# Sliding-window attention inside a weight-streaming trunk: one transposed tile for two triangles of probabilities, three banks for the queries, and sums, scaling and masks on GpSimd

## The chip, the cores and the metric

One Trainium2 chip, one of its cores. The kernel is launched once. The metric is the device time in microseconds of one execution; what stands as "time" is the median over several runs, and one further execution was taken by the profiler. The engines are named as the profile names them: PE is TensorE's matrix products and PEld its weight loads, DVE is VectorE, ACT is ScalarE, POOL is GpSimd, SP issues the DMAs.

## What is computed

Two layers over 256 tokens of width 2048: a recurrent layer with its feed-forward part, then one projection to shared keys and values, then an attention layer with its feed-forward part. The change lies in the attention. Cut to that:

```python
SEQ, D_MODEL, HEAD_DIM, N_HEADS, N_KV_HEADS, WINDOW, BLOCK = 256, 2048, 64, 32, 4, 128, 128

def attn_block(x, g, w_q, q_g, sinks, w_o, k_band, v_band):
    h = rms_norm(x, g)
    q = rms_norm((h @ w_q).reshape(bsz, s, N_KV_HEADS, GROUP, HEAD_DIM), q_g)
    scores = einsum("bnqhgd,bnkhd->bnhgqk", q, k_band) / sqrt(HEAD_DIM)
    scores = where(mask, scores, NEG_INF)      # 0 <= q_pos - k_pos < 128, k_pos exists
    probs = softmax(concatenate([scores, sink], -1), -1)[..., :-1]
    out = einsum("bnhgqk,bnkhd->bnqhgd", probs, v_band)
    return x + out.reshape(bsz, s, N_HEADS * HEAD_DIM) @ w_o
```

With 256 tokens there are two blocks of 128 queries. Queries of block 0 see their own block's keys up to themselves: a lower triangle. Queries of block 1 see their own block's lower triangle and, of block 0's keys, those fewer than 128 back: the strictly upper triangle. The two triangles of block 1 fill a 128x128 square between them without overlap.

## The kernel before

**The products.** All weights stream from HBM in jobs of 128x1024 float32 (two k-tiles of 128 by four feature tiles of 128). ACT rounds a job to `hi` (L259), DVE forms the remainder `lo` (L260), and PE adds `hi`·x_hi, `hi`·x_lo and `lo`·x_hi into PSUM (`products`, L289 to 325). A product of 128 columns of weights with 256 tokens is called narrow here; a job is 24 narrow products. Where a feature tile owns a whole PSUM bank of 512 columns ("wide"), one 512-column product can do `hi`·x_hi and `hi`·x_lo at once; `products` places runs of three of those at chosen points (after other work on PE, and in jobs named by `SYNC`). There are 704 jobs. Buffers are four deep, and the split of a job is emitted three jobs ahead (`stream`, L271).

**Groups and banks.** PSUM has eight banks. `group` (L340) runs the jobs of four feature tiles and then hands the banks to `done`, which empties them. For the queries (`w_q`, four groups of eight jobs) a group holds four banks, three of them wide (`wide=3`). For the first two groups of `w_o` four feature tiles share two banks (`paired`) and the jobs of both groups are interleaved: six jobs of the first, six of the second, then two and two (`late=2`, L492 to 505).

**The attention visits.** Everything beside the job stream is generators that `run_bg` steps between half jobs (a tick is half a job). `pairs` (L926 to 977) makes *visits*: 16 pairs of heads pass through a pipeline, each pair being two heads of 64 rows in one 128-partition tile. In a visit PE does up to three things for three different pairs, in this order: V, the product of values with transposed probabilities (`values`, L861); T, the transposes of probabilities (`transposes`, L873, six of 128x128); S, the scores (`scores`, L881). A pair has its scores in visit i, its transposes in visit i+2 and its values in visit i+3. All these go through `pe_other` (L327). Between them, `softmax` (L892) runs on DVE and ACT: masked maximum (L900), exponentials with their sums, the reciprocal of the sum, and four scalings on DVE (`ts`, L131), two per head. After T, ACT copies the transposes from PSUM into two tiles (a 128x512 and a 128x256 copy). A visit takes up to four banks from the eight, at most `MISC` = 4 may be out, and none starts while `hold` is set, which is in a group's last two jobs (L360). When the job stream needs a result that is not there (`need`, L213), it steps the generators until it is, with no job between.

**The queries' finish.** The task in `attn` (L987 to 1031) squares the queries, sums them per head on PE, transposes, computes the scales, and queues four pairs per group.

## Time and profile before

| | |
|---|---|
| median of 3 runs | 1990.1 us (1989.94 to 1990.55) |
| profiled execution: span | 1988.6 us |
| PE busy / PEld busy | 1982.0 us (100%) / 1935.5 us (97%) |
| DVE busy | 1271.2 us (64%) |
| ACT busy | 1067.9 us (54%) |
| POOL busy | 0.2 us, 4 instructions |
| HBM read | 371.88 MB, 188 GB/s over the span |

The execution's own device time beside its span is not listed; the median stands 1.5 us above the span, which is the part of an execution that lies outside the first and the last instruction. In the span's 40 slices PE shows nine tenths or more in each and the granted PE clock is full in each. The attention stage, from the first scores to the last values, lies at about 1072 to 1210 us. Matmul rows overlap in the trace, so what a product costs is read from the distance between the starts of two rows and not from the length of one.

### The profile page before, as it was taken

The numbers are of one execution on the slowest core, as the hardware profiler recorded it, in microseconds if no ns is written. First come the engines' busy times: TensorE is split into PE (matmuls) and PEld (weight loads), VectorE is DVE, ScalarE is ACT, GpSimd is POOL, SyncE is SP. The second block draws the span as 40 slices with busy tenths as digits, with TensorE's granted clock in tenths as the row PEclk, the third lists the DMA queues.
The fourth block names the chain that finished last, engine by engine and source line by source line (L and its number), as shares of the span: only waits on it lengthen the run. The fifth ranks groups of instructions, "written<-read, shape, count | busy, mean of one in ns | idle before, by whom it ended". The sixth has DMA issues, their size and how long they took to land.

```text
span 1988.6 us, 40066 instructions
## 1 busy us (share of the span) xinstructions
PE 1982.0 (100%) x16684; PEld 1935.5 (97%) x16684; DVE 1271.2 (64%) x2049; ACT 1067.9 (54%) x1624; POOL 0.2 (0%) x4
## 2 busy tenths in 40 slices
PE   9999999999999999999999999999999999999999
PEld 9999999999999999999999889999999999999999
DVE  8988876556556655545668786755565565554453
ACT  7798655444444444444556775544454454444442
POOL 0000000000000000000000000000000000000000
PEclk9999999999999999999999999999999999999999
DMA  8555655565556555556555435565566656656663
GB/s 279 185 187 182 211 191 192 196 196 191 192 195 196 191 192 196 195 191 194 197 186 167 134 101 163 188 197 195 191 193 196 195 191 194 197 193 203 204 208 128
DMA packets 105302, 376.58 MB, mean 189 GB/s; under 512 B 11808, under 2 KB 14240, under 8 KB 105120
## 3 DMA queue, kind: packets, MB, share of 16 engines
q1 hardware_dynamic: 104832, 373.88, 57.8%
q8 instruction: 130, 2.13, 0.4%
q14 instruction: 52, 0.43, 0.1%
q10 hardware_dynamic: 288, 0.14, 0.0%
HBM read 371.88 MB, written 2.10 MB: 188 GB/s over the span
## 4 chain that ended last, share of the span: by engine, by line
PE 99%; ACT 0%; DVE 0%; DMA 0%; issue 0%; ACTq 0%
PE b L323 94%; PE b L334 2%; PE b L641 1%; PE b L331 1%; PE b L832 1%; ACT s L113 0%; PE b L321 0%; PE b L841 0%; PE b L842 0%; PE b L843 0%; DMA x<-in_x 0%; DVE s L131 0%; DVE lo L260 0%; ACT L113 0%; DVE s L122 0%
## 5 line engine op out<-in xcount | busy, mean ns | idle before, releaser
L323 PE MATMUL b<-s,hi 128*128 128x256 f32 (+1 forms) x10276 | 1431.9, 285 | 0.4 <-ACT s L113 0.4
L323 PEld LDWEIGHTS b<-s,hi 128*128 128x128 f32 x10276 | 1313.4, 188 | 30.4 <-ACT s L113 0.7
L260 DVE TENSOR_TENSOR lo<-raw,hi 128x1024 fp32r<-128x1024 f32 (+1 forms) x705 | 861.4, 1223 | 651.2 <-ACT hi L259 648.1
L259 ACT ACTIVATE hi<-raw 128x1024 fp32r<-128x1024 f32 (+1 forms) x705 | 745.7, 1059 | 817.7 <-PE b L323 756.7
L323 PE MATMUL b<-s,lo 128*128 128x256 f32 x5504 | 831.8, 277 | 0.0
L323 PEld LDWEIGHTS b<-s,lo 128*128 128x128 f32 x5504 | 720.4, 188 | 2.4 <-issue 0.8
L113 ACT ACTIVATE s<-h 128x256 fp32r<-128x256 f32 (+1 forms) x106 | 40.8, 411 | 23.8 <-DVE h L122 23.8
L113 ACT ACTIVATE t<-b 128x256 f32<-128x256 f32 x136 | 49.8, 374 | 2.5 <-PE b L323 0.3
L113 ACT ACTIVATE s<-x,par 128x256 fp32r<-128x256 f32 x80 | 38.6, 499 | 19.3 <-DVE x L122 13.6
L113 ACT ACTIVATE s<-s 128x256 f32<-128x256 f32 (+1 forms) x112 | 39.6, 409 | 5.7 <-DVE s L126 5.5
L113 ACT ACTIVATE h<-h 128x256 f32<-128x256 f32 (+1 forms) x104 | 38.8, 375 | 2.1
L113 ACT ACT_TABLE_LOAD x30 | 38.5, 1283 | 0.5
L126 DVE SCALAR_TENSOR_TENSOR s<-x,par,s 128x256 fp32r<-128x256 f32 x80 | 37.5, 482 | 1.4 <-ACT s L113 0.8
L122 DVE TENSOR_TENSOR h<-b,rstd 128x256 f32<-128x256 f32 x100 | 37.6, 417 | 0.0
L122 DVE TENSOR_TENSOR x<-x,b 128x256 f32<-128x256 f32 x64 | 24.1, 418 | 21.0 <-PE b L323 21.0
L113 ACT ACTIVATE s<-s,h 128x128 f32<-128x128 f32 x64 | 28.3, 443 | 13.3 <-DVE h L131 13.2
L122 DVE TENSOR_TENSOR h<-h,rstd 128x256 f32<-128x256 f32 x94 | 35.4, 419 | 0.0
L122 DVE TENSOR_TENSOR h<-h,h 128x256 f32<-128x256 f32 x88 | 35.0, 420 | 0.4 <-ACT h L113 0.4
L122 DVE TENSOR_TENSOR s<-h,s 128x256 fp32r<-128x256 f32 x88 | 35.2, 420 | 0.1
L122 DVE TENSOR_TENSOR h<-b,t 128x256 f32<-128x256 f32 x92 | 34.6, 417 | 0.0
L122 DVE TENSOR_TENSOR s<-s,s 128x256 fp32r<-128x256 f32 (+1 forms) x80 | 30.9, 422 | 3.5 <-ACT s L113 3.5
L334 PE MATMUL b<-s,s 64*128 64x256 f32 (+3 forms) x292 | 29.0, 302 | 0.1
(99 smaller groups left out, 566.4 us busy)
## 6 DMA issues: line engine op xcount, KB each, us to landing
raw<-in_ffn_in SPq DMA_DIRECT2D x352, 512.0 KB, 3.5
raw<-in_ffn_out SPq DMA_DIRECT2D x176, 512.0 KB, 4.3
raw<-in_lru_in SPq DMA_DIRECT2D x63, 512.0 KB, 3.6
raw<-in_lru_out SPq DMA_DIRECT2D x32, 512.0 KB, 3.7
raw<-in_w_q SPq DMA_DIRECT2D x32, 512.0 KB, 3.3
raw<-in_w_o SPq DMA_DIRECT2D x32, 512.0 KB, 3.3
raw<-in_gate SPq DMA_DIRECT2D x8, 512.0 KB, 3.9
raw<-in_kv SPq DMA_DIRECT2D x8, 512.0 KB, 4.3
```

Source lines behind the costliest of these rows:

```text
L113: self.nc.scalar.activation(out, in_, func, **kw)
L122: self.nc.vector.tensor_tensor(out, a, b, op)
L126: self.nc.vector.scalar_tensor_tensor(out, a, s, b, op0, op1)
L259: self.nc.scalar.activation(hi[:, q], raw[:, q], AF.Copy)
L260: self.nc.vector.tensor_tensor(lo[:, q], raw[:, q], hi[:, q].bitcast(F32), ALU.subtract)
L323: self.nc.tensor.matmul(*args, **kw)
L331: self.other = self.ins(f(*args, **kw))
L334: self.other = self.ins(f(*args, **kw))
L641: nc.tensor.matmul(out[j], (hi if high else lo)[:, c:c + P], x2[kt][:, q:q + T], start=kt == 0 and high > q, stop=kt == 1 and not high)
L832: nc.tensor.matmul(ps[f][:, 0:T], w0, x2[kt][:, q:q + T], start=k0 + kt == 0 and high > q, stop=k0 + kt == ND - 1 and not high)
```

## The change

It has seven parts, all in the attention stage.

1. **One tile for two triangles.** After the exponentials, POOL adds the two halves of block 1 (columns 128 to 255 and 256 to 383) into the first of them, for each head (L925 of the changed kernel). The four scalings move from DVE to POOL, each now 128x128 (L929). `transposes` makes four transposes rather than six.
2. **Masks after the transposes.** ACT copies one 128x512 tile from PSUM rather than that and a 128x256 one. POOL multiplies its block-1 half by two 0/1 masks from the constants (L971): once into a second tile (own block), once in place (previous block). Both are products of 128x256 elements. V reads both tiles.
3. **Order in a visit.** V, S, T where it was V, T, S. The pacing credits to `run_bg` go from 900/700/900 to 800/900/450 ns.
4. **Even visits.** While pairs are still to come, a visit waits for a new pair rather than running with the old ones alone.
5. **Three banks.** `w_q` groups use two wide banks and one bank shared by the other two feature tiles (`packed`); `MISC` goes to 5, and `hold` is set for one job before the end of a packed group and not at all in a paired one.
6. **`w_o` interleaved.** The jobs of its first two groups alternate one by one.
7. **Constants.** 256 more columns (the two masks).

```diff
-K_HS, K_MASK = 640, 672
-NCON = 672 + 384
+K_HS, K_MASK = 640, 672
+K_PREV, K_OWN = 672 + 384, 672 + 512
+NCON = 672 + 640
...
-    MISC = 4
+    MISC = 5
...
+                    elif packed:
+                        ps = [self.bank() for _ in range(3)]
+                        st["ps"] = [(ps[0], True, 0, 1), (ps[1], True, 1, 1)]
+                        st["ps"] += [(ps[2][:, f * T:f * T + T], False, 2, f) for f in range(2)]
+                        st["bank"] = ps
...
-                elif c >= nk // 2 - 2:
+                elif c >= nk // 2 - (1 if packed else 2) and not paired:
                     self.hold = True
...
-                    n = nk // 2 - late
-                    self.jobs += first[0][:n] + first[1][:n] + first[0][n:] + first[1][n:]
+                    self.jobs += [j for both in zip(*first) for j in both]
...
             for hh in (1, 0):
-                for j in (2, 1, 0):
-                    o = ps[0][:, hh * T + j * P:hh * T + j * P + P] if j < 2 else ps[1][:, hh * P:hh * P + P]
+                for j in (1, 0):
+                    o = ps[0][:, hh * T + j * P:hh * T + j * P + P]
                     self.pe_other(o, sc[hh][:, j * P:(j + 1) * P], one, f=nc.tensor.transpose)
...
             for hh in range(2):
-                for b, c0, c1 in blocks:
+                o = sc[hh][:, P:2 * P]
+                nc.gpsimd.tensor_tensor(o, o, sc[hh][:, 2 * P:3 * P], ALU.add)
+                for b in range(2):
                     i = b * 2 + hh
-                    o = sc[hh][:, c0:c1]
-                    self.ts(o, o, den[:, i:i + 1], None, ALU.mult)
+                    o = sc[hh][:, b * P:b * P + P]
+                    nc.gpsimd.tensor_scalar(o, o, den[:, i:i + 1], None, ALU.mult)
...
-                elif not (A or B or C):
+                elif n < ND or not (A or B or C):
                     yield 1
                     continue
...
                     values(A[0], A[1], pt[1])
-                    self.pe(900)
+                    self.pe(800)
+                if new:
+                    scores(new[0], new[1], ps)
+                    self.pe(900)
                 if B:
                     transposes(B[1], pt)
-                    self.pe(700)
-                if new:
-                    scores(new[0], new[1], ps)
-                    self.pe(900)
+                    self.pe(450)
...
                     self.a(s[0], pt[0])
-                    self.a(s[1][:, 0:T], pt[1][:, 0:T])
+                    for o, c in ((last, K_OWN), (dst, K_PREV)):
+                        m = con[:, c:c + P].unsqueeze(1).broadcast_to([P, 2, P])
+                        nc.gpsimd.tensor_tensor(o, dst, m, ALU.mult)
```

In the programs' instruction order, a full visit on PE before, in the third group of `w_q`. Rows whose product reads two `s` tiles and writes 64 rows are V, those that read `con` are T, those with 128 rows from `s_11041` are S; those with `hi` or `lo` are the job stream.

```order
L323 MATMUL b_90<-s_11180,lo_82 128x256
L331 MATMUL b_86<-s_11935,s_11045 64x256
L334 MATMUL b_86<-s_11935,s_11045 64x256
L334 MATMUL b_86<-s_11936,s_11045 64x128 x2
L334 MATMUL b_86<-con,s_11792 128x128
L334 MATMUL b_85<-con,s_11792 128x128 x2
L334 MATMUL b_86<-con,s_11791 128x128
L334 MATMUL b_85<-con,s_11791 128x128 x2
L334 MATMUL b_87<-s_11041,s_11628 128x128
L334 MATMUL b_84<-s_11041,s_11628 128x128
```

The same place on the same engine in the changed program: V, then the last of the twelve score products, then T, then the job stream.

```order
L335 MATMUL b_89<-s_12217,s_11045 64x128 x2
L335 MATMUL b_90<-s_11042,s_11977 128x128
L335 MATMUL b_83<-s_11042,s_11977 128x128
...
L335 MATMUL b_90<-s_11042,s_11977 128x256
L335 MATMUL b_83<-s_11042,s_11977 128x256
L335 MATMUL b_84<-con,s_12140 128x128 x2
L335 MATMUL b_84<-con,s_12139 128x128 x2
L324 MATMUL b_86<-s_11240,hi_77 128x256 x2
```

Six transposes into two banks have become four into one, and they stand between the scores and the job stream rather than between values and scores.

On POOL, which before had no instruction of the attention, each visit now gives it eight. The rows of one period: two masks for the pair that was just transposed (L971), then for the pair whose exponentials are running two sums (L925) and four scalings (L929), then the next visit's masks.

```order
L971 TENSOR_TENSOR s_12217<-s_12216,con 128x256
L971 TENSOR_TENSOR s_12216<-s_12216,con 128x2x128
L925 TENSOR_TENSOR s_12224<-s_12224 128x128
L925 TENSOR_TENSOR s_12225<-s_12225 128x128
L929 TENSOR_SCALAR s_12224<-s_12224,h_96 128x128 x2
L929 TENSOR_SCALAR s_12225<-s_12225,h_96 128x128 x2
L971 TENSOR_TENSOR s_12302<-s_12301,con 128x256
L971 TENSOR_TENSOR s_12301<-s_12301,con 128x2x128
```

On DVE these four rows are gone from each softmax.

```order
L131 TENSOR_SCALAR s_12149<-s_12149,h_95 128x128
L131 TENSOR_SCALAR s_12149<-s_12149,h_95 128x256
L131 TENSOR_SCALAR s_12150<-s_12150,h_95 128x128
L131 TENSOR_SCALAR s_12150<-s_12150,h_95 128x256
```

In the first jobs of `w_o`, PE before: the last products of one visit's scores are followed at once by the values of the next visit, without a job between. There are three such doubled visits, with 24 narrow products between one double and the next.

```order
L334 MATMUL b_83<-s_11043,s_12243 128x256
L334 MATMUL b_85<-s_11043,s_12243 128x256
L334 MATMUL b_87<-s_12790,s_11045 64x256 x2
L334 MATMUL b_87<-s_12791,s_11045 64x128 x2
L334 MATMUL b_87<-con,s_12676 128x128
```

In the changed program 36 narrow products stand between the transposes of one visit and the values of the next in this stage:

```order
L335 MATMUL b_90<-con,s_12740 128x128 x2
L324 MATMUL b_89<-s_12306,hi_78 128x256 x4
L324 MATMUL b_84<-s_12221,lo_82 128x256 x2
...
L324 MATMUL b_85<-s_12567,lo_79 128x256 x2
L332 MATMUL b_83<-s_13005,s_11045 64x256
```

Over the whole stage there are as many visits as before, 19. In the changed program no two touch: between one visit's last product and the next one's first lie 36 narrow products (twelve times), 48 (three times, across a group's end) or 72 (three times, with the next queries' sums between). In `w_q`, where 9 visits fell before, 11 now fall. The runs of three wide products from the first queries' sums to the end of `w_q` are 19 where they were 32.

More of the change, by code (lines that the diff above doesn't have):

```diff
@@ L338, in ins, with group @@
         return getattr(i, "ins", i)
-    def group(self, src, nk, xs, done, last=False, sync=(), paired=False, jobs=None, wide=2):
+    def group(self, src, nk, xs, done, last=False, sync=(), paired=False, jobs=None, packed=False):
         st = {}
@@ L353, in mm @@
                         st["bank"] = ps
+                    elif packed:
[3 more added lines that the diff above has]
+                        st["bank"] = ps
                     else:
                         ps = [self.bank() for _ in range(4)]
-                        st["ps"] = [(p, bool(sync) and f < wide, f, 1) for f, p in enumerate(ps)]
+                        st["ps"] = [(p, bool(sync) and f < 2, f, 1) for f, p in enumerate(ps)]
                         st["bank"] = ps
@@ L378, in mm @@
                     todo = [(k, f, p) for g, q in order for k in range(2) for f in g for p in q]
-                self.products(todo, st, hi, lo, x2, c == nk // 2 - 1, keep, paired)
+                self.products(todo, st, hi, lo, x2, c == nk // 2 - 1, keep, paired or packed)
                 if last:
@@ L490, in residual, with project @@
         self.spawn(task())
-    def project(self, w, nk, xs, gains, r, out=None, late=0):
+    def project(self, w, nk, xs, gains, r, out=None, late=False):
         first = [[], []]
@@ L1032, in done @@
                 self.spawn(task())
-            self.group(lambda c, g=g: w[g, c], ND, xs, done, g == 3, self.SYNC, wide=3)
-        self.project(self.d["w_o"], ND, at, gains, rn, late=2)
+            self.group(lambda c, g=g: w[g, c], ND, xs, done, g == 3, self.SYNC, packed=True)
+        self.project(self.d["w_o"], ND, at, gains, rn, late=True)
     def run(self):
@@ L1092, in constants @@
     con[:, K_MASK:K_MASK + 384] = np.concatenate([own, prev, own], axis=1)
+    con[:, K_PREV:K_PREV + P] = prev.T == 0
+    con[:, K_OWN:K_OWN + P] = own.T == 0
     return con
```

3 lines of the change are left out of this document (added).

## The prediction

> **What bounds the kernel now.** I read the page first, then the chain that ended last, then windows of the attention stage, then PE's timeline of single visits, and last the costs by form.
>
> ```profile
> span 1988.6 us, 40066 instructions
> PE 1982.0 (100%) x16684; PEld 1935.5 (97%) x16684; DVE 1271.2 (64%) x2049; ACT 1067.9 (54%) x1624; POOL 0.2 (0%) x4
> PE 99%; ACT 0%; DVE 0%; DMA 0%; issue 0%; ACTq 0%
> ```
>
> PE carries 99% of the chain. What lies beside PE is hidden; a microsecond of PE saved or added anywhere is a microsecond of the result. So the question is how long PE spends on attention visits, and whether anything new makes it wait there.
>
> ```profile
> 76.91 21.76 PE b L323 x192
> 1198.31 4.24 PE b L323 x36
> ```
>
> Two pieces of the chain, with start, length and count. In the job stream a narrow product costs 21.76/192 = 0.1133 us; in the attention stage, after other work on PE, 4.24/36 = 0.1178 us. So there are two paces 4.5 ns apart. 704 jobs of 24 narrow products are 16896 x 0.1133 = 1914 us, which the change leaves alone; about 75 us are open to discussion.
>
> ```profile
> 1093.00:1124.00 31.00, 30.94 (x241) 26.06 (x241) 23.21 (x74) 23.67 (x60) 0.00 (x0) 1.00 0.42 137
> 1155.00:1189.00 34.00, 32.23 (x298) 27.08 (x297) 28.91 (x121) 26.84 (x85) 0.00 (x0) 1.00 0.25 79
> 1189.00:1210.00 21.00, 21.00 (x184) 18.89 (x183) 12.56 (x32) 12.05 (x31) 0.00 (x0) 1.00 0.42 132
> ```
>
> Windows: length, then busy time of PE, PEld, DVE, ACT, POOL. In the middle window, the doubled visits at the start of `w_o`, DVE is busy 28.91 of 34 us and PE misses 1.8 us: there PE waits for DVE. In `w_q` DVE has 23.21 of 31 us (75%).
>
> **What a visit costs.** PE's timeline: start, length, line, form.
>
> ```profile
> 1106.27 0.43 PE L331 MATMUL b<-s,s 128*64 128x256 f32 x1
> ...
> 1107.07 0.88 PE L334 MATMUL b<-con,s 128*128 128x128 f32 x6
> 1107.88 0.96 PE L334 MATMUL b<-s,s 64*128 64x128 f32 x12
> 1108.77 0.50 PE L321 MATMUL b<-s,hi 128*128 128x512 f32 x1
> 1109.11 0.40 PE L323 MATMUL b<-s,hi 128*128 128x512 f32 x1
> ...
> 1196.63 0.43 PE L331 MATMUL b<-s,s 128*64 128x256 f32 x1
> ...
> 1197.44 0.87 PE L334 MATMUL b<-con,s 128*128 128x128 f32 x6
> 1198.07 0.71 PE L323 MATMUL b<-s,hi 128*128 128x256 f32 x4
> ...
> 1208.33 0.43 PE L331 MATMUL b<-s,s 128*64 128x256 f32 x1
> ...
> 1209.13 0.74 PE L323 MATMUL b<-s,hi 128*128 128x256 f32 x4
> ...
> 1077.63 0.32 PE L331 MATMUL b<-s,s 64*128 64x128 f32 x1
> ...
> 1078.52 0.50 PE L321 MATMUL b<-s,hi 128*128 128x512 f32 x1
> ...
> 1088.23 0.27 PE L331 MATMUL b<-con,s 128*128 128x128 f32 x1
> ...
> 1088.97 0.96 PE L334 MATMUL b<-s,s 64*128 64x128 f32 x12
> 1089.86 0.50 PE L321 MATMUL b<-s,hi 128*128 128x512 f32 x1
> ```
>
> From start to start: a full visit takes 2.50 us, V 0.80, T 0.81, S 0.89. V alone takes 0.80 and S alone 0.89, so those two are the same by themselves. T is not: followed by S it takes 0.81 (0.74 without V), followed by the job stream 1198.07 - 1197.44 = 0.63, which is six times 0.105. So T into S costs 0.11 to 0.18 for the turn, T into the job stream nothing. S into the job stream costs a further 0.11: after 1108.77 the next 512-column product comes 0.34 later, where two narrow products' time is 0.23. An old full visit is thus 2.61 us.
>
> **The change, part by part.**
>
> *Two transposes fewer and the new order.* New visit: V 0.80, S 0.89, T 4 x 0.105 = 0.42, and a turn from S into T. No row shows V into S or S into T. S into T lies between 0, if the turn is already in S's 0.89, and the 0.18 seen between T and S; I take the 0.11 that S costs before the job stream, because T has the job stream's shape (128*128) and follows or precedes it free. V into S lies between 0 and another 0.2 beyond V's 0.80. I take 0, since V's 0.80 already holds a turn into a full-array product. New full visit 2.22 us, bounds 2.1 to 2.5; saved 0.39, bounds 0.1 to 0.5. Thirteen full visits: 13 x 0.39 = **5.1 us**. The one visit with T and S alone goes from 1.63 + 0.11 to 0.89 + 0.11 + 0.42: **0.3 us**. The two with V and T alone lose two transposes each: **0.4 us**.
>
> *Even visits.* The three doubles now:
>
> ```profile
> 1160.77 0.43 PE L331 MATMUL b<-s,s 128*64 128x256 f32 x1
> ...
> 1165.75 2.15 PE L323 MATMUL b<-s,hi 128*128 128x256 f32 x16
> ...
> 1168.77 0.43 PE L331 MATMUL b<-s,s 128*64 128x256 f32 x1
> ...
> 1170.68 0.87 PE L334 MATMUL b<-con,s 128*128 128x128 f32 x6 [1.04 <-DVE s L131]
> ...
> 1175.36 2.16 PE L323 MATMUL b<-s,hi 128*128 128x256 f32 x16
> ...
> 1178.39 0.43 PE L331 MATMUL b<-s,s 128*64 128x256 f32 x1
> ...
> 1183.85 2.15 PE L323 MATMUL b<-s,hi 128*128 128x256 f32 x16
> ```
>
> They take 4.98, 6.59 and 5.46 us, with 0.11 after each: 17.36. Six single old visits would be 15.66. The transposes there wait for DVE's scaling (the 1.04 us is one such wait). With at least 36 narrow products, 36 x 0.1133 = 4.1 us, between visits, the excess of **1.7 us** goes. Interleaving `w_o` moves no work: each pair's result is needed 36 products or more after its values are made.
>
> *Three banks, fewer wide ones.* The number of products is the same. The runs of three wide products, after which the quicker pace returns, fall from 32 to 19 in the `w_q` stage, and the visits there rise from 9 to 11. If all of the stage's 516 narrow products from the first queries' sums on ran at the slow pace, that would be 516 x 0.0045 = 2.3 us; some of this is paid already. I take **+0.6 us**, bounds 0 and 1.5.
>
> *Off PE.* DVE loses four scalings in each softmax, ACT one copy per visit. Both are hidden now and stay so; the cover is PE's 4.1 us between visits, and the `lo` splits run two jobs ahead of their use. The larger constants are 128 KB more in SP's one DMA of them at job 8, under PE's stream; SP's queue is otherwise as before.
>
> *POOL, the new link.* A pair goes: scores, DVE, ACT, reciprocal on DVE, two sums and four scalings on POOL, T two visits later, copy on ACT, two masks on POOL, then V of the next visit. PE is in order: V waiting for a mask holds S, T and the job stream. The times:
>
> ```profile
> 1130.76 0.43 PE L331 MATMUL b<-s,s 128*64 128x256 f32 x1
> ...
> 1138.89 0.18 DVE L137 RECIPROCAL h<-h 128x4 f32<-128x4 f32 x1
> ```
> ```profile
> L260 DVE TENSOR_TENSOR lo<-raw,hi 128x1024 fp32r<-128x1024 f32 x35 | 42.8, 1222 | 7.5 <-ACT hi L259 6.1 <-PE b L334 1.4
> L113 ACT ACTIVATE s<-b 128x512 f32<-128x512 f32 x16 | 9.4, 587 | 0.0
> L131 DVE TENSOR_SCALAR s<-s,h 128x128 f32<-128x128 f32 x32 | 9.1, 284 | 0.5
> L122 DVE TENSOR_TENSOR s<-s,s 128x256 fp32r<-128x256 f32 x12 | 4.6, 424 | 0.4 <-ACT s L113 0.4
> ```
>
> Now the reciprocal is done 8.3 us after its visit begins. S comes 0.8 us earlier in a new visit (1.69 rather than 2.50 us at its end): 7.5 us. The next visit begins at 2.22 + 4.1 = 6.3, its copy is done at about 6.3 + 2.22 + 0.3 + 0.59 = 9.4 (0.3 for the way from PE to ACT, an estimate), and its masks, which stand behind the scalings in POOL's queue, must be done by 12.6, when the visit after it begins. No row prices POOL. By DVE's rows, 0.284 for a scaling and 0.424 for a mask, the chain is 7.5 + 4 x 0.284 = 8.6, then from 9.4 two masks to 10.3: 2.3 us to spare. Let POOL be q times as slow as these rows: 7.5 + q x (1.14 + 0.85) reaches 12.6 at q = 2.6. All of a period's work on POOL, with two sums at 0.284, is q x 2.55 us and fills a period of 6.3 us at q = 2.5. So up to about q = 2.4 this costs nothing. As the far bound I take DVE's operation on 128x1024, four times a mask's size: 1.222/0.424 gives q = 2.9. Between q = 1 and 2.9 I take a value below 2, nearest to the rows of the same shape, and allow **0.5 us** in all for chance waits.
>
> The Trainium skill (GPSIMD Engine Reference, § 3.1 Elementwise) gives a 2048-element fp32 addition as 1.96 times as long on GpSimd as on VectorE; by that, as an estimate, q would be 2 and the chain would end 1.1 us before PE needs it, so the sum would stand. No run here shows it yet.
>
> **The sum.** 5.1 + 0.3 + 0.4 + 1.7 - 0.6 - 0.5 = 6.4 us off the profiled 1988.6: 1982.2. The median lies 1.5 us above that execution's span: **1983.5 us**, 0.33% less. Its own range is 1980 (turns free, pace unchanged) to 1986.
>
> **Rivals.**
>
> *POOL is late (slower).* Place: the first V product of each visit that follows 36 narrow products, ten of them. What speaks for it: DVE's `lo` has two operands in SBUF and runs 1.5 times per period for 1.222 us each; if POOL cannot read while DVE does that, one mask or scaling waits up to 1.2 us, and the room of 12.6 - 7.5 = 5.1 us for 1.99q shrinks to 3.9, so that q = 2 is already the limit. Against it: the `lo` splits fall mostly where POOL waits for the exponentials. Once POOL fills the period, the period is 2.55q: at q = 2.9 it is 7.4 us, 1.1 us of waiting at each of ten visits, 11 us in all, and 1983.5 - 0.5 + 11 = **1994 us**. It outweighs the whole gain from q = 2.75 on (7.0 us of stalls), the same as before; slower by 0.2% from 2.9.
> The Trainium skill (SBUF — State Buffer, § SBUF: two separate sides) states such a rule: GpSimd and a VectorE operation with two SBUF inputs take a shared port pair in turn, and the loser blocks for the whole instruction. By it the reduced room above applies. The trace of before, with POOL idle, can't show it.
>
> *The turns cost the same and the groups' ends wait.* If changing the array's use costs what it did, only the two transposes go: a full visit saves 0.21, thirteen 2.7 rather than 5.1. And the visit 12 products after a group's end (three times) puts its scores into banks that DVE has just emptied: two adds of 0.42, perhaps behind a `lo` of 1.22, against 12 x 0.1133 + 0.80 = 2.2 us; up to 0.6 us each. Together 2.4 + 1.8: **1987.7 us**. For it: DVE at 75% there. Against: it has four scalings less to do per visit.
>
> *The change doesn't even out what PE waits for.* The stalls of 1.7 us move to other visits, the rest holds: **1985.2 us**.
>
> **How the numbers follow.** Forecast 0.60, POOL late 0.20 (about 0.12 of it beyond +0.2%, the rest within), turns and groups' ends 0.12, stalls moved 0.08. A measurement of this kernel tells 0.2%, 4 us, from no change: faster means under 1986.1, slower over 1994.1. Faster: 0.60 + 0.08 + a quarter of the 0.12 = 0.71; slower 0.12; within 0.17. The range runs from 1980 to 1989.5: it holds the forecast, the moved stalls, the dear turns and the mild part of POOL's lateness.
>
> **What would show it.** Right: a full visit of 2.2 us from V to the job stream; no PE wait on DVE's scaling; 36 products between visits; POOL's masks ending before V's first product; 64 transposes of probabilities on PE where there were 96. Wrong: PE waiting at V with POOL as releaser, visits of 3 us and more, or DVE's `lo` lengthened where POOL works; then the first rival holds. If visits take 2.4 us, the turns were mis-sized.

## The result, and the profile after

| | before | after |
|---|---|---|
| time, median of 11 runs each | 1990.52 us (1989.93 to 1992.39) | 1986.19 us (1985.44 to 1987.02) |
| ratio of the times | | 0.9979, 95% interval 0.9971 to 0.9987 |
| span of the profiled execution | 1988.6 us | 1985.0 us |

The change saves 0.21%, where 0.33% was forecast; no execution of the one kernel reaches those of the other. Of the saving that the prediction worked out, the larger part arrived, and some 3.7 us of it were spent again on new waits. First the page of the changed kernel (span, busy times, chain of waits), which answers to the first fence of the prediction.

```profile
span 1985.0 us, 40177 instructions
PE 1976.7 (100%) x16691; PEld 1934.5 (97%) x16691; DVE 1259.8 (63%) x1981; ACT 1063.6 (54%) x1608; POOL 94.0 (5%) x132
PE 97%; ACT 1%; DVE 1%; POOL 1%; issue 0%; DMA 0%; ACTq 0%; POOLq 0%
```

PE still carries the chain, but 97% rather than 99% of it, and POOL has a share. POOL's 94.0 us all lie in the attention stage. The windows of that stage, with the columns as before (length, then busy PE, PEld, DVE, ACT, POOL, then the granted PE clock):

```profile
1093.00:1124.00 31.00, 30.39 (x256) 26.65 (x254) 22.12 (x73) 22.55 (x62) 21.95 (x30) 1.00 0.39 125
1155.00:1189.00 34.00, 32.90 (x302) 29.68 (x300) 24.68 (x76) 26.66 (x75) 24.67 (x34) 1.00 0.39 125
1189.00:1210.00 21.00, 20.31 (x178) 18.43 (x179) 10.68 (x23) 11.06 (x24) 13.34 (x18) 1.00 0.48 142
```

Before, PE was short of its window only in the middle one, by 1.8 us. Now it misses 0.6, 1.1 and 0.7 us. DVE is relieved (24.68 against 28.91 in the middle window), and POOL is busy for about 70% of the first two. What PE waits for, in the view of waits (us in total, times, longest):

```profile
PE b L332 <- POOL s L971: 2.9, 4, 1.0
```

These are the first products of V, waiting for POOL's masks. PE's timeline shows a visit without and one with such a wait:

```profile
1108.02 0.43 PE L332 MATMUL b<-s,s 128*64 128x256 f32 x1
...
1109.70 0.66 PE L335 MATMUL b<-con,s 128*128 128x128 f32 x4
1110.11 0.48 PE L322 MATMUL b<-s,hi 128*128 128x512 f32 x1
1110.43 1.57 PE L324 MATMUL b<-s,hi 128*128 128x512 f32 x10
...
1115.17 0.43 PE L332 MATMUL b<-s,s 128*64 128x256 f32 x1 [0.61 <-POOL s L971]
```

V and S take 1109.70 - 1108.02 = 1.68 us, T 0.41, and the first 512-column product 0.32, which is 0.09 more than two narrow ones. A new full visit is 2.18 us against 2.61. Over the 19 visits, those that took longer than an unhindered one of their kind lost about 3.7 us together (worked out visit by visit from PE's single rows; the largest are 1.1 us at 1189, 0.76 at 1202, 0.68 at 1115 and 0.67 at 1149, all of them ahead of V). Without these the span would be 1981.3 us. This 1981.3 is the base of the ledger below.

Why POOL is late shows in the timeline of all engines ahead of the longest of these waits:

```profile
1183.08 3.32 POOL L929 TENSOR_SCALAR s<-s,h 128x128 f32<-128x128 f32 x4
...
1183.54 1.23 DVE L261 TENSOR_TENSOR lo<-raw,hi 128x1024 fp32r<-128x1024 f32 x1 [0.57 <-ACT hi L260]
...
1186.37 2.55 POOL L971 TENSOR_TENSOR s<-s,con 128x256 f32<-128x256 f32 x2
...
1187.13 1.21 DVE L261 TENSOR_TENSOR lo<-raw,hi 128x1024 fp32r<-128x1024 f32 x1
...
1188.97 0.43 PE L332 MATMUL b<-s,s 128*64 128x256 f32 x1 [1.02 <-POOL s L971]
```

Four scalings take 3.32 us, two masks 2.55, and a `lo` split of DVE runs inside each stretch. The costs by form on POOL, all rows of the program, and the split beside them:

```profile
L929 POOL TENSOR_SCALAR s<-s,h 128x128 f32<-128x128 f32 x64 | 52.7, 839 | 0.0
L971 POOL TENSOR_TENSOR s<-s,con 128x256 f32<-128x256 f32 x32 | 27.5, 858 | 10.6 <-ACT s L114 9.3
L925 POOL TENSOR_TENSOR s<-s 128x128 f32<-128x128 f32 x32 | 14.5, 458 | 1100.7 <-ACT s L114 1094.5 <-PE b L335 6.2
L261 DVE TENSOR_TENSOR lo<-raw,hi 128x1024 fp32r<-128x1024 f32 x35 | 43.4, 1239 | 13.0 <-ACT hi L260 12.9
```

The means hide two populations. Of the 64 scalings, 29 lie clear of every `lo` split and take 601 ns on average; 33 overlap one by over 0.1 us and take 1063 on average, 1859 at most. Of the 32 masks 25 are clear (740 ns) and 7 overlap (1278, at most 1755). The longest rows exceed the clear ones by 1.26 and 1.02 us; a split takes 1.22.

This can be carried through to the waits. Ahead of each of the four, POOL goes from its first scaling to its last mask without a pause of over 0.1 us, and the operations that a split held up there exceed their clear lengths by 0.99, 0.98, 1.98 and 1.74 us together (at 1115, 1149, 1189 and 1202, from POOL's single rows). The waits are 0.61, 0.60, 1.02 and 0.69 us, less each time. By this sum POOL, at its clear prices, would have been done before V.

### The profile page after: what moved, and what is told of

Its sections match the earlier page's. It is cut to its first block, busy times and chain, and to the rows that moved or that the text cites. A ratio compares the mean times of both kernels' runs of the same rounds, so it can differ in the third digit from the quotient of the medians.

```text
span 1985.0 us, 40177 instructions
## 1 busy us (share of the span) xinstructions
PE 1976.7 (100%) x16691; PEld 1934.5 (97%) x16691; DVE 1259.8 (63%) x1981; ACT 1063.6 (54%) x1608; POOL 94.0 (5%) x132
## 4 chain that ended last, share of the span: by engine, by line
PE 97%; ACT 1%; DVE 1%; POOL 1%; issue 0%; DMA 0%; ACTq 0%; POOLq 0%
PE b L324 93%; PE b L646 1%; ACT s L114 1%; PE b L335 1%; PE b L837 1%; PE b L332 1%; DVE s L905 0%; POOL s L929 0%; ACT hi L260 0%; DMA x<-in_x 0%; PE b L847 0%; PE b L846 0%; PE b L848 0%; DVE lo L261 0%; POOL s L971 0%
## 5 line engine op out<-in xcount | busy, mean ns | idle before, releaser
L925 POOL TENSOR_TENSOR s<-s 128x128 f32<-128x128 f32 x32 | 14.5, 458 | 1100.7 <-ACT s L114 1094.5
L929 POOL TENSOR_SCALAR s<-s,h 128x128 f32<-128x128 f32 x64 | 52.7, 839 | 0.0
L123 DVE TENSOR_TENSOR x<-x,b 128x256 f32<-128x256 f32 x64 | 24.2, 417 | 21.2 <-PE b L324 21.2
L123 DVE TENSOR_TENSOR h<-b,rstd 128x256 f32<-128x256 f32 x100 | 37.6, 416 | 0.0
L123 DVE TENSOR_TENSOR s<-s,s 128x256 fp32r<-128x256 f32 (+1 forms) x80 | 32.0, 431 | 5.6 <-ACT s L114 5.4
L123 DVE TENSOR_TENSOR h<-h,rstd 128x256 f32<-128x256 f32 x94 | 35.4, 418 | 0.0
L123 DVE TENSOR_TENSOR s<-h,s 128x256 fp32r<-128x256 f32 x88 | 35.1, 420 | 0.2 <-ACT s L114 0.2
L123 DVE TENSOR_TENSOR h<-h,h 128x256 f32<-128x256 f32 x88 | 34.9, 418 | 0.4 <-ACT h L114 0.4
```

The lines of the kernel that those rows point to most:

```text
L123: self.nc.vector.tensor_tensor(out, a, b, op)
L925: nc.gpsimd.tensor_tensor(o, o, sc[hh][:, 2 * P:3 * P], ALU.add)
L929: nc.gpsimd.tensor_scalar(o, o, den[:, i:i + 1], None, ALU.mult)
```

## The experiments

Eleven kernels. The names of lines are those of the changed kernel where nothing else is said. "Scalings", "sums", "masks" are L929, L925, L971.

### Scalings back on DVE

```diff
+                for b, c0, c1 in blocks:
+                    i = b * 2 + hh
+                    o = sc[hh][:, c0:c1]
+                    self.ts(o, o, den[:, i:i + 1], None, ALU.mult)
                 nc.gpsimd.tensor_tensor(o, o, sc[hh][:, 2 * P:3 * P], ALU.add)
-                    nc.gpsimd.tensor_scalar(o, o, den[:, i:i + 1], None, ALU.mult)
```

> The four scalings of each softmax go back to DVE, in the shapes they had before; sums and masks stay on POOL. Theory A (PE waits because POOL's chain of scalings and masks fills its period: 4 x 0.58 + 2 x 0.44 + 2 x 0.78 us start to start, and more when a lo split on DVE holds it up): PE's waits on POOL, 3.7 us in the changed kernel, vanish, and the time falls from 1986.2 to between 1982.3 and 1983.5 us. Theory B (the waits have another cause that POOL only happens to end last, such as the exponentials or the emptying of banks): they stay, and the time is within 0.7 us of 1986.2. Theory C (DVE, with the scalings back, becomes what PE waits for): PE waits on DVE by 2 us or more, 1985 to 1987 us.

Measured 1992.04 us (1990.29 to 1994.47), ratio to before 1.0013 (1.0004 to 1.0021). All three ranges are missed, that of theory A by over 8 us. C's sign, PE waiting on DVE by 2 us or more, is there; A's, that the waits on POOL vanish, is not. The profiled execution took 1994.47 us, 2.4 above the median. The view of waits on PE:

```profile
PE b L335 <- DVE s L123: 3.2, 3, 1.4
PE b L332 <- POOL s L971: 2.5, 1, 2.5
```

The first is a wait that I had set aside: the visit 12 narrow products after a group's end puts its scores into banks that DVE has to empty (L123), and DVE is late with that. From the timeline of this place:

```profile
1090.78 0.40 DVE L123 TENSOR_TENSOR s<-b,t 128x256 f32<-128x256 f32 x1
...
1091.10 1.00 DVE L132 TENSOR_SCALAR s<-s,h 128x128 f32<-128x128 f32 x4
1091.24 0.32 PE L335 MATMUL b<-s,s 64*128 64x128 f32 x1 [1.38 <-DVE s L123]
...
1092.01 0.42 DVE L123 TENSOR_TENSOR s<-b,t 128x256 f32<-128x256 f32 x1
...
1092.49 1.64 PE L335 MATMUL b<-s,s 64*128 64x128 f32 x11 [0.93 <-DVE s L123]
```

Between two emptyings stand the four scalings, 1.00 us, and the second wait, 0.93 us, ends with the emptying behind them. The first, 1.38 us, ends with the emptying at 1090.78; what stands in front of that one is the reciprocal, for which DVE had waited 0.89 us on ACT's exponentials.

The wait on POOL is one of 2.5 us, at the last visit, though POOL has only sums and masks left:

```profile
1202.47 3.23 POOL L929 TENSOR_TENSOR s<-s 128x128 f32<-128x128 f32 x2 [3.16 <-DVE s L132]
...
1205.66 2.38 POOL L971 TENSOR_TENSOR s<-s,con 128x256 f32<-128x256 f32 x2
...
1208.10 0.65 PE L332 MATMUL b<-s,s 128*64 128x256 f32 x1 [2.51 <-POOL s L971]
```

L929 is the sum in this kernel. Two sums take 3.23 us where two clear ones take 0.92, and two masks 2.38 rather than 1.48; three `lo` splits, at 1202.70, 1204.17 and 1205.83, run beside them. The 3.2 us above the clear lengths are more than the wait. So POOL can be late with little work, where splits follow one another.

The waits named are 5.7 us, yet the span was 1992.7, 11.4 above the base. The rest is in the granted clock, the third column from the right in these windows:

```profile
1092.12:1098.95 6.83, 6.46 (x28) 5.73 (x29) 5.74 (x16) 4.73 (x11) 2.43 (x4) 0.50 0.28 93
1208.17:1211.59 3.42, 3.42 (x18) 2.73 (x19) 0.42 (x1) 0.98 (x2) 0.22 (x1) 0.50 0.64 214
```

After the waits PE runs on at half clock. One minus the clock, times the window, is 3.4 + 1.7 = 5.1 us. 5.7 + 5.1 = 10.8 of the 11.4 us are accounted for.

### One scaling per head as a 128x256 product on POOL

```diff
-                for b in range(2):
-                    i = b * 2 + hh
-                    o = sc[hh][:, b * P:b * P + P]
-                    nc.gpsimd.tensor_scalar(o, o, den[:, i:i + 1], None, ALU.mult)
+                o = sc[hh][:, 0:2 * P].rearrange("p (b q) -> p b q", b=2)
+                m = den[:, hh:hh + 3:2].unsqueeze(2).broadcast_to([P, 2, P])
+                nc.gpsimd.tensor_tensor(o, o, m, ALU.mult)
```

> POOL keeps the scaling, but as one product of 128x256 with the reciprocals broadcast per head in place of two 128x128 scalings by a per-partition scalar. Theory A: POOL's work per visit falls from 4.8 to about 4.0 us of unhindered time (two instructions of 0.74 us for four of 0.58 us) and half as many instructions can meet a lo split; PE's waits on POOL fall from 3.7 us to under 1.5 us and the time to between 1982.5 and 1984.5 us. Theory B: within 0.7 us of 1986.2 us. If the broadcast operand makes the instruction slow (over 1.2 us), A expects no gain.

Measured 1984.48 us (1983.92 to 1985.03), ratio 0.9973 (0.9963 to 0.9983), at the upper end of what was expected. The view of waits:

```profile
PE b L332 <- POOL s L970: 0.5, 1, 0.5
```

and its scaling among the costs by form:

```profile
L928 POOL TENSOR_TENSOR s<-s,h 128x256 f32<-128x256 f32 x32 | 30.8, 984 | 0.6 <-DVE s L123 0.3
```

The masks' wait falls from 2.9 to 0.5 us when POOL's scaling work falls from 52.7 to 30.8 us and nothing else in the program changes. POOL's lateness is thus what cost the changed kernel its waits. This experiment doesn't part the length of the work from the meetings: those fall too, from 33 scalings that overlap a split to 23 products. Clear of the splits, this product takes 613 ns for twice the elements of a scaling that takes 601. The two are different operations, so it isn't shown how much of the gain comes from having half as many instructions.

### V, T, S rather than V, S, T

In the changed kernel the blocks for S and T in a visit change places.

> The changed kernel with the transposes ahead of the scores again (V, T, S). Turn theory: a full visit without waits takes 2.38 us or more from V to the job stream rather than 2.10, plus 0.02 after it (0.25 to 0.35 us more over thirteen visits, 3 to 4.5 us), of which the longer period gives POOL some room, so 1987.5 to 1990 us. Rival (order within a visit costs nothing, the visit got shorter only by its two transposes): a full visit of the same length as in the changed kernel, and a time within 0.7 us of 1986.2.

Measured 1990.43 us (1989.63 to 1991.43), ratio 1.0003 (0.9994 to 1.0012). A visit without wait on PE:

```profile
1108.73 0.43 PE L332 MATMUL b<-s,s 128*64 128x256 f32 x1
...
1109.53 0.66 PE L335 MATMUL b<-con,s 128*128 128x128 f32 x4
1110.12 0.95 PE L335 MATMUL b<-s,s 64*128 64x128 f32 x12
1111.00 0.50 PE L322 MATMUL b<-s,hi 128*128 128x512 f32 x1
1111.34 1.57 PE L324 MATMUL b<-s,hi 128*128 128x512 f32 x10
```

T followed by S takes 0.59 where T followed by the job stream takes 0.41. The visit is 2.27 + 0.11 = 2.38 against 2.18: the order alone is worth 0.20 x 13 = 2.6 us. The rest of the loss is a mask wait of 1.83 us at 1184.89, with this behind it:

```profile
1185.00:1189.00 4.00, 4.00 (x26) 2.89 (x27) 0.95 (x4) 2.79 (x11) 2.46 (x5) 0.57 0.43 135
```

The clock again, 0.43 x 4 = 1.7 us. The rival (the order costs nothing, within 0.7 us of 1986.2) failed; the turn theory's range was exceeded by 0.4 us, while a visit cost 0.20 us more and not 0.25 to 0.35. Ahead of the long wait one scaling and one mask were held up, by 0.98 and 0.84 us above their clear lengths, together as long as the wait. S is later in this order by T's 0.59 us, and with it the exponentials, the sums and scalings and the masks behind them; that this is what moves them under the splits was not tried.

### The changed schedule with the old probabilities

The changed visits, banks and order of jobs, but four scalings on DVE, six transposes, two copies and no POOL work.

```diff
-                for j in (1, 0):
+                for j in (2, 1, 0):
...
-                    for o, c in ((last, K_OWN), (dst, K_PREV)):
-                        nc.gpsimd.tensor_tensor(o, dst, m, ALU.mult)
+                    self.a(s[1][:, 0:T], pt[1][:, 0:T])
```

> The changed kernel's schedule (V, S, T; even visits; three banks; w_o interleaved) with the probabilities handled as before: six transposes, two copies by ACT, scaling on DVE, nothing on POOL. If even visits remove the waits of the doubled visits and POOL is what spoils the changed kernel: full visits of about 2.4 us, no PE wait over 0.5 us, 1985.0 to 1987.0 us, that is about as fast as the changed kernel although it transposes 32 tiles more. Rival (even visits only move the waits elsewhere): PE waits of 1.5 us or more on DVE's scaling, and 1987.5 us or more.

Measured 1990.53 us (1989.27 to 1991.79), ratio 1.0002 (0.9993 to 1.0011). Full visits without a wait take 0.23 us more than those of the changed kernel, two transposes' time, as expected. The waits are those of the first experiment:

```profile
PE b L335 <- DVE s L123: 2.8, 4, 0.9
```

and the window behind the first two of them, 0.78 and 0.93 us in one visit:

```profile
1093.62:1097.04 3.42, 3.42 (x14) 3.04 (x13) 3.42 (x14) 2.91 (x7) 0.00 (x0) 0.50 0.47 153
```

The time failed the theory and fell to its rival, though what PE waits for is the emptying of banks and not the scalings themselves. So the new schedule, taken alone as it stands, gives nothing: its waits are at the visits close behind a group's end.

### The new probabilities on the old schedule

The kernel before with parts 1, 2 and 7 of the change alone.

> The kernel before with parts 1 and 2 of the change alone: four transposes, sums, scalings and masks on POOL, but V, T, S, doubled visits, four banks and w_o in blocks of six jobs as before. Theory (POOL's chain is long, so it needs even visits): the 32 transposes save 3.5 us, but each visit that follows another one directly waits for two masks behind a copy and for POOL's scalings; the doubled visits take 3 us or more each beyond what they take now and the time is 1993 to 2005 us, slower than the kernel before. Rival (even visits are not needed; the gain comes from the transposes): 1986 to 1988 us.

Measured 2001.61 us (2000.78 to 2002.11), ratio 1.0058 (1.0045 to 1.0071). This is inside the wide range expected. The doubled visits leave POOL no time; the view of waits:

```profile
PE b L335 <- POOL s L967: 3.6, 2, 2.7
```

and a window behind one of the waits:

```profile
1181.00:1185.00 4.00, 4.00 (x21) 3.88 (x19) 1.86 (x10) 1.35 (x3) 2.53 (x5) 0.53 0.01 4
```

PE's named waits in the stage are 8.6 us, on POOL, DVE and ACT, and the clock is at half for 17.1 us in two stretches (1174.5 to 1184.8 and 1191.6 to 1198.4), 8.5 us lost. Each half of the change alone is worse than the whole; as they stand, neither saves anything by itself.

### A third mask per visit on POOL

```diff
-                    for o, c in ((last, K_OWN), (dst, K_PREV)):
+                    for o, c in ((spare, K_OWN), (last, K_OWN), (dst, K_PREV)):
```

> The changed kernel with a third mask product of 128x256 on POOL per visit, ahead of the other two, into a spare half tile that nobody reads. Theory (POOL's chain ends last): its 0.74 us per visit appear at the visits that wait now and at some that just don't: PE's waits on POOL grow by 4 to 9 us, and the time is 1990 to 1997 us. Rival (POOL's lateness is chance, at a few visits, with room elsewhere): under 1988 us.

Measured 1994.36 us (1992.12 to 1994.92), ratio 1.0019 (1.001 to 1.0027), as expected.

```profile
PE b L332 <- POOL s L972: 8.6, 6, 2.3
```

One product of 0.74 us (clear) more per visit brings 5.7 us of waits more. With the experiment that shortens POOL's work, this shows POOL's period from both sides: the changed kernel stands at its edge.

### `lo` in two halves

In the attention stage (jobs 376 to 423) DVE's split is two instructions of 128x512 rather than one of 128x1024; once in the changed kernel, once with POOL's 128x256 scaling.

```diff
-            self.nc.vector.tensor_tensor(lo[:, q], raw[:, q], hi[:, q].bitcast(F32), ALU.subtract)
+            m = 512 if 376 <= i < 424 else n
+            for e in range(c, c + n, m):
+                q = slice(e, e + m)
+                self.nc.vector.tensor_tensor(lo[:, q], raw[:, q], hi[:, q].bitcast(F32), ALU.subtract)
```

> The changed kernel with the lo split of the 48 jobs of w_q and of the first two groups of w_o in two 128x512 instructions on DVE in place of one 128x1024; the same arithmetic. Theory (a POOL instruction that meets a lo split waits until that one instruction is over): POOL instructions that now take up to 1.86 us take at most about 1.4 us, the mean of POOL's scalings falls from 839 to under 780 ns, PE's waits on POOL fall by 1 us or more, and the time is 1984.3 to 1985.7 us, although DVE pays 0.16 us more per job. Rival (POOL and DVE share bandwidth, or the long POOL instructions have another cause): the same lengths of POOL instructions as now, and 1986 us or more.

> The last one and the broadcast scaling (one 128x256 product per head) together. Theory: both shorten POOL's chain, by 0.85 us and by part of the blocked time; the waits left with the broadcast scaling alone (about 1.6 us, at four visits) fall to 0.5 us or less: 1983.2 to 1984.2 us, the fastest of all. Rival (what is left there are waits on DVE's emptying of banks at group ends): no gain over 1984.5 us.

Measured 1988.85 us (1987.95 to 1989.25), ratio 0.9993 (0.9984 to 1.0002), and 1988.82 (1988.15 to 1989.12), ratio 0.9993 (0.9985 to 1.0002): 2.7 and 4.3 us worse than the kernels they were made from, where both were to be better. The halves did only in part what they were meant to do to single instructions: the longest mask fell from 1755 to 1221 ns, the longest scaling from 1859 to 1580, but the mean of the scalings stayed at 839 where under 780 was expected. 35 scalings still overlap a split (mean 1032 ns), and the waits move:

```profile
PE b L335 <- POOL s L974: 3.1, 5, 1.6
PE b L335 <- ACT h L114: 1.8, 2, 1.0
```

and with the 128x256 scaling

```profile
PE b L338 <- DVE s L123: 2.0, 2, 1.1
```

beside two waits on ACT (1.9 us together) and one on POOL (0.7). Why the halves bring so little shows in the first of the two kernels, ahead of a wait on POOL of 0.59 us:

```profile
1110.00 3.31 POOL L932 TENSOR_SCALAR s<-s,h 128x128 f32<-128x128 f32 x4
1110.47 1.30 DVE L264 TENSOR_TENSOR lo<-raw,hi 128x512 fp32r<-128x512 f32 x2 [0.58 <-ACT hi L260]
```

Four scalings still take 3.31 us: the one that meets the two halves takes 1.57 us, 0.97 more than a clear one, and ends behind the second half. With the whole split it was 0.99 more at this place. The halves follow each other without a pause, and the scaling is held for both. A delay longer than POOL's own operation, 1.26 us on a scaling of 0.60, does not look like two engines that share a rate and fits a lock; that the lock ends with each instruction is not shown by the halves. Why they make ACT's and DVE's own work later is not settled; the two halves cost DVE 2 x 725 = 1450 ns (means of the costs by form) where one split cost 1239, which is one part of it.

### The visit after a group's end put off

The first experiment and the schedule alone pointed to the same spot. Here a visit may not start in the first job after a three-bank group, so that 24 products or more stand in between; with the scalings on DVE, with the old probabilities, and with POOL's 128x256 scaling.

```diff
-                    self.hold = False
+                    self.hold = packed and self.hold
+                elif packed and c == 1:
+                    self.hold = False
```

> As e1_scale_dve (the four scalings on DVE, sums and masks on POOL), but a visit may not start in the first job after the end of a group with three banks, so that 24 to 36 narrow products rather than 12 lie between the group's end and the next visit. Theory (the visit after a group's end waits because its scores go into banks that DVE has not emptied, DVE's scalings standing ahead of the emptying): 12 or more products, 1.4 us or more, are added to the room, so the 3.7 and 1.4 us at those visits go, PE's wait on DVE at line 123 falls under 1 us, and the time falls by 3 to 5 us to 1987 to 1989; below that only if the 2.5 us wait for masks at the last visits goes too. Rival (DVE as a whole has no room with the scalings, wherever the visit stands): the waits turn up at the next visits, time 1990.5 or more. The last values come 36 products later, where the first interleaved w_o job that needs them stands; a wait there would show as PE waiting on ACT or POOL at the last visit and the job behind it.

> As e4_sched (the changed visits, banks and order of jobs, but the old probabilities: scalings on DVE, six transposes, two copies), with the same delay of the visit after a group's end. In this program one visit moves by 84 products from the one before it, and gets the squares of the queries' sums with it. Theory: the 2.1 and 1.5 us at the visits after a group's end go, PE's wait on DVE at line 123 falls from 2.8 us to under 1, time 1986.5 to 1988. Rival (the waits come from DVE's load as a whole): 1990 or more.

> As e2_scale_tt (the scaling as one 128x256 product with a spread operand per head on POOL), with the same delay of the visit after a group's end. In e2_scale_tt the two visits after a group's end lost 0.58 and 0.22 us. Theory: those 0.8 us go and nothing takes their place: 1983.3 to 1984.2. Rival (the last visit, now directly ahead of the w_o jobs that use its values, makes the job stream wait for the copy of its values): 1984.5 to 1986.

Measured 1987.72 us (1986.94 to 1988.17), ratio 0.9987 (0.9978 to 0.9996); 1986.83 (1986.3 to 1987.62), ratio 0.9984 (0.9975 to 0.9994); and 1983.30 (1983.18 to 1983.79), ratio 0.9966 (0.9953 to 0.9978). All three times lie in the ranges of the theory. With the scalings on DVE one expectation failed, a wait on L123 below 1 us:

```profile
PE b L324 <- DVE s L123: 1.9, 1, 1.9
PE b L332 <- POOL s L973: 1.4, 2, 1.2
```

DVE's timeline ahead of the 1.9 us:

```profile
1120.75 1.01 DVE L132 TENSOR_SCALAR s<-s,h 128x128 f32<-128x128 f32 x4
1121.67 1.22 DVE L261 TENSOR_TENSOR lo<-raw,hi 128x1024 fp32r<-128x1024 f32 x1
1122.81 0.42 DVE L123 TENSOR_TENSOR s<-b,s 128x256 fp32r<-128x256 f32 x1
```

Here the job stream itself waits for the bank, behind scalings and a split: the same queue, met at another place. With the old probabilities the wait on L123 is gone, and two short waits on ACT (0.8 us together) are what PE loses in this stage. The third, POOL's shorter scaling with the late visit, is faster than both kernels of the study (2.9 us faster than the changed one); in its window of the doubled visits' old place PE misses nothing:

```profile
1155.00:1189.00 34.00, 34.00 (x313) 30.98 (x312) 25.19 (x79) 25.09 (x65) 18.89 (x25) 1.00 0.44 141
```

The second of the three says more than its time: with those visits put off, the schedule with the old probabilities comes to 1986.83, within 0.7 us of the changed kernel's 1986.19, with nothing on POOL. Most of what the whole change saves can be had from the schedule alone, once the visits after a group's end stand later.

### The ledger

Span = base 1981.3 + longer visits (0.20 or 0.23 for each of 13 to 16 visits with T) + PE's named waits in the attention stage + clock lost there (one minus the granted clock, times the window).

| kernel | longer visits | waits | clock | sum | span |
|---|---|---|---|---|---|
| scalings on DVE | 0 | 5.7 | 5.1 | 1992.1 | 1992.7 |
| 128x256 scaling on POOL | 0 | 0.7 | 0 | 1982.0 | 1983.2 |
| V, T, S | 2.6 | 3.9 | 1.7 | 1989.5 | 1989.6 |
| schedule alone | 3.7 | 2.8 | 1.7 | 1989.5 | 1989.4 |
| third mask | 0 | 8.6 | 1.7 | 1991.6 | 1992.8 |
| `lo` in halves | 0 | 4.9 | 0 | 1986.2 | 1986.9 |
| `lo` in halves, 128x256 scaling | 0 | 4.6 | 0 | 1985.9 | 1986.3 |
| scalings on DVE, late visit | 0 | 3.7 | 0 | 1985.0 | 1985.3 |
| schedule alone, late visit | 3.7 | 0.8 | 0 | 1985.8 | 1984.8 |
| 128x256 scaling, late visit | 0 | 1.1 | 0 | 1982.4 | 1982.0 |

Ten kernels with spans up to 10.8 us apart come out within 1.2 us. The new probabilities on the old schedule are left out, since their visits are the old ones. The base comes from the changed kernel itself, with all 3.7 us taken off; its named waits alone, 2.9, would put it at 1984.2, and it measured 1985.0.

## Why the prediction was right, and where it was not

**What bounds the kernel.** "A microsecond of PE saved or added anywhere is a microsecond of the result" held, with one addition that it lacked: a microsecond of PE's waiting can cost nearly two, by the clock.

**A full visit.** Predicted 2.22 us, measured 2.18, so 13 x 0.43 = 5.6 us rather than 5.1. The bounds (2.1 to 2.5) held. In detail the turns lie elsewhere: V and S together take 1.68, so S into T costs nothing where 0.11 was taken, and T before the job stream 0.09 after its last product where nothing was taken. "T has the job stream's shape" was half right: T into S costs 0.18, as the old rows showed.

**Even visits.** The excess of 1.7 us went: no doubled visit is left, and PE waits for no scaling on DVE. The experiment with the new probabilities on the old schedule adds what the prediction did not say: with POOL in the chain, the other parts (3 to 6) together are worth 15.4 us, 2001.61 against 1986.19. Which of them does it was not parted.

**Pace.** Predicted +0.6 us; from start to start, narrow products that follow one another took 5.50 us above 0.1133 each in the whole program before and 6.05 after, +0.55. The runs of three wide products were miscounted: a recount gives 35 before and 22 after, not 32 and 19; their difference, and so the term, stays.

**POOL: the step that failed.** "I take a value below 2, nearest to the rows of the same shape, and allow 0.5 us in all for chance waits." The prices were not far off: clear of splits, 601/284 gives q = 2.1 for a scaling and 740/424 gives 1.75 for a mask. By the condition "up to about q = 2.4 this costs nothing" there would have been no wait. The prediction's own sign against it, "PE waiting at V with POOL as releaser", is what the trace shows. The error is the ground on which the first rival was put aside: "the `lo` splits fall mostly where POOL waits for the exponentials." They do not; 33 of 64 scalings met one, and 28 of the 35 splits in the stage met POOL. Counting the waits for it, a scaling has q = 2.95 and a mask 2.0, and the rival's sentence that with the lock "q = 2 is already the limit" was the right one. The term measured 3.7 us, 3.3 of it ahead of V and the rest at a group's end and ahead of the queries' sums. That is 3.2 more than allowed and more than the whole difference of 2.7 between the predicted 1983.5 and the measured 1986.19; the cheaper visit gave some of it back. The result lies just above the forecast's own range (to 1986) and inside the wide one, in the part that was kept for the mild form of this rival.

The Trainium skill (SBUF — State Buffer, § SBUF: two separate sides) says that GpSimd and a VectorE operation with two SBUF inputs hold a shared port pair in turn, each for the whole instruction. The trace agrees for whole splits: the longest delay is the length of one, 1.26 us against 1.22. Between the halves of a split, two instructions, the scaling did not get in. DVE is held up in turn: in the best kernel the 24 splits that meet POOL take 1354 ns on average and 1810 at most, against 1226 over all 705 of the program. The Trainium skill (GPSIMD Engine Reference, § 3.1 Elementwise) gives 1.96 for an addition; here it is 1.75 for a mask and 2.1 for a scaling.

**The rivals.** POOL late came true in kind, not in size: 1994 was worked out for q = 2.9 with a full period, and POOL's work (two sums, four scalings and two masks at their means: 0.92 + 3.36 + 1.72) now fills 6.0 of the 6.4 us from one unhindered V to the next (1101.59 to 1108.02). The third mask per visit takes it over the edge, at 1994.36. The groups' ends cost the changed kernel only about 0.24 us (S at 1123.90), but the two variants that leave the scalings on DVE lose 3.2 and 2.8 us in waits there, and the clock behind them: "it has four scalings less to do per visit", named against this rival, fits that: they are the kernels where it does not hold. That stalls move to other visits was right as well, though by POOL and not by DVE.

**The sum.** 5.6 + 0.3 + 0.4 + 1.7 - 0.55 - 3.7 = 3.75 us off the profiled span; 3.6 measured. The forecast's last step has a slip: 1982.2 + 1.5 is 1983.7 and not 1983.5. And the 1.5 is too small: in each listed execution of both kernels the time is 1.74 to 1.85 us above the span.

## What to carry to other kernels

When work is moved to an engine that shares something with a busy one, count how often their instructions meet before pricing it by its length alone; here what the meetings added to POOL's rows exceeds each wait, while its clear prices would have fitted. Cutting an instruction in two that then run back to back did not help. Moving work and evening out the schedule can each lose alone and win together, so test them in both combinations, and look at what stands in front of the emptying of a bank that the next stage needs: putting off the visits there gave the schedule alone most of what the whole change saves. A wait on PE should be priced with the clock behind it: waits of 1.7 us in all, within one visit, cost as much again.

## What the runs showed of the hardware

**Half clock after short waits.** In the experiments with V, T, S, with the schedule alone and with the third mask, one place each lost 1.7 us to the granted clock after waits of 1.83, of 0.78 and 0.93 close together, and of 2.35 us; this is 3.4 us at half clock each time. It does not follow from the length of a single wait: the 1.90 us on L123 in the kernel with the scalings on DVE and the late visit left the clock at 1.00,

```profile
1118.62:1122.03 3.41, 2.77 (x21) 2.45 (x19) 1.63 (x7) 3.41 (x13) 0.59 (x1) 1.00 0.52 154
1122.03:1125.45 3.42, 2.17 (x15) 2.08 (x16) 3.42 (x14) 1.58 (x5) 3.04 (x4) 1.00 0.40 122
1125.45:1128.86 3.41, 3.41 (x30) 2.79 (x31) 2.78 (x9) 3.41 (x15) 0.44 (x1) 1.00 0.32 106
```

and so did every wait of the changed kernel, none of which was over 1.1 us. These windows are not chosen freely. In each trace the changes of the granted clock lie whole steps of 3.413 us apart (in the kernel with the scalings on DVE the two drops, at 1092.12 and 1208.17, are 34 steps apart), so each run can be laid out in such steps; above, the wait falls into two of them, with 0.65 and 1.25 us without PE. Over the attention stage of all thirteen kernels, the seven steps at full clock in which PE did nothing for 1.48 to 2.72 us were each followed by half clock, and no step with 1.38 us or less was. The Trainium skill (TensorE: Matmul & The Clock Gate, § What's actually happening) has a window of about 3.4 us that runs freely and halves the clock after an idle one. The length and the free run agree; that PE must be idle for a whole window does not. By these steps the limit lies between 1.38 and 1.48 us, about 0.4 of a window, but this is not the whole rule: at the end of two kernels steps with 1.6 and 1.8 us left the clock at full, and why some stretches last two or three steps is open.

**POOL's prices.** Clear of the splits: 601 ns for a 128x128 scaling by a value per partition, 459 for a 128x128 sum, 613 for a 128x256 product with a spread operand, 740 for a 128x256 product with a mask. One spread product cost what one scaling of half its size did; from the sum to the products twice the size cost 0.15 to 0.28 us more.
